# LayerNorm of a convolution module in one sweep per half, weight splits issued at other places, the last convolution behind the first products of the next matrix

## The chip, the cores and the metric

The kernel runs on one core of one Trainium2 chip. The metric is the device time of one execution in microseconds. One profiled execution of the kernel before is read here; its times are counted from the first instruction of the span.

## What is computed

A two-layer decoder trunk on 512 tokens of width 1024, all in float32. Layer 0 is a mixer, layer 1 a causal Conformer convolution module; each is followed by a convolutional feed-forward (FFN). The change lies in the convolution module of layer 1:

```python
def conformer_conv(h, pw1_w, pw1_b, dw_w, dw_b, ln_g, ln_b, pw2_w, pw2_b):
    a, g = jnp.split(h @ pw1_w + pw1_b, 2, axis=-1)
    y = a * jax.nn.sigmoid(g)
    y = causal_depthwise_conv(y, dw_w, dw_b)            # 31 taps
    y = jax.nn.silu(layer_norm(y, ln_g) + ln_b)         # over the 1024 features
    return y @ pw2_w + pw2_b
# then: x = x + gate * y, a modulated RMSNorm, and the FFN of layer 1
```

## The kernel before

**Layout.** Activations stand feature-major: eight blocks k = 0..7 of 128 features by 512 tokens. The tokens are two halves h = 0, 1 of 256. The LayerNorm works on transposed tiles, `zt[h][i]`: half h, pair i of the feature blocks 2i and 2i+1, as 2 groups (a) of 128 tokens by 256 features.

**Matrix products.** Every float32 product is made of three passes of a rounded high part and a rest (`mm3`, lines 190 to 192). Activations are split into `hi` and `lo` (ACT copies, DVE subtracts). Weights come 1024 rows by 256 columns at a time, in a fixed order of the stream: the eight of pw1, the four of pw2 (called W0 to W3 here), then the FFN's. `pull_raw` loads one as two halves of 512 KB into nine `raw` buffers over SP's queue; `pull_split` (lines 257 and 259) splits one into `whi`/`wlo` (four buffers each, two to a weight) or, with an argument, into `shi`/`slo` in general slots. `next_w(ahead=n)` hands out the next weight and first splits n more.

**The convolution.** `glu_out(k, ...)` forms the gated block `yd` (ACT sigmoid, DVE line 1230) and copies it shifted into `y8` by 16 small DMAs, eight on SP's queue and eight on POOL's (line 1239). `conv_pe(k, h)` does the 31 taps as 64 small matmuls (line 1259) and ends with a DVE add that evacuates the PSUM tile (line 1262). `stat(k)` transposes on TensorE (1269), ACT copies into `zt` (1271), and DVE makes `bn_stats` (1276). The last two blocks, `LAST = (6, 7)`, go by halves of the tokens (lines 1306 to 1329).

**LayerNorm and pw2** (lines 1377 to 1397). `ln_stats(h)` is a chain of small DVE steps that ends with mean and 1/sqrt of the variance. `ln_pair(h, i)` normalises pair i (two DVE operations, line 1356), transposes it back on TensorE (line 1360, tile `zb`), and makes silu (ACT, 1364), `hi` (ACT, 1367) and `lo` (DVE, 1368) for blocks 2i and 2i+1. `pw2_first(h, k)` is block k's share of the products with W0 and W1: 12 matmuls of 256 columns into four PSUM tiles. The loop over n does pair n, and then the products of pair n-1. After it `proj_out` uses W2 and W3, adds the residual, and goes on to the FFN.

**Order.** TensorE's instructions run in the order in which the program writes them, throughout. DVE and ACT keep the written order inside the block of lines 1377 to 1397; outside it a scheduler of the compiler places their instructions, and it also puts instructions written behind the block between those of the block. SP's loads are placed by the scheduler too. Each engine's queue is served in order.

Of the kernel before, what the change touches and what calls it, by code (L numbers as in the profile page):

```python
# [13 lines left out]
ALU = mybir.AluOpType  # L14
# [3 lines left out]
P = 128  # L18
D = 1024
KT = 8  # L20
# [15 lines left out]
CD = (3, 3, 3, 3, 3, 3)  # L36
# [20 lines left out]
def body(ctx, tc, x, c, positions, ada_w, ada_b, norm_mix_g, norm_ffn_g, ab_w_in, a_vnorm_g,  # L57
# [4 lines left out]
    V, A, PE = nc.vector, nc.scalar, nc.tensor  # L62
# [162 lines left out]
    raws, parts = [], []  # L225
# [38 lines left out]
    def pull_split(ks_slots=0):  # L264
        for _ in split_steps(ks_slots):
            pass

    taken = [0]
# [29 lines left out]
    def later(n, f):  # L298
        cnt[0] += 1
        due.append((now[0] + n, cnt[0], f))  # L300
# [661 lines left out]
    def drain(*its):  # L962
        for it in its:
            for _ in it:
                pass
# [253 lines left out]
    z0 = {}  # L1219
# [32 lines left out]
    def conv_pe(k, h=None):  # L1252
        n, i = (256, 0) if h is None else (128, 128 * h)
        cps = psum([P, 2, n], "cv")
        for q in range(4):
            o = 4 * q if not h else 0
            for s in range(8):
                g = 32 * (s % 4)
                PE.matmul(cps[g:g + 32, s // 4, o:], wds[k][q][:, 32 * s:32 * s + 32],  # L1259
                          y8[k][s // 2][:, s % 2, i + o - 4 * q:i + n - 4 * q],  # L1260
                          start=(q == 0 and s < 4), stop=(q == 3 and s > 3), tile_position=(0, g))
        V.tensor_tensor(z0[k][:, :, i:i + n], cps, cdb[:, 2 * k:2 * k + 2, None].to_broadcast([P, 2, n]), op=ALU.add)

    def stat(k, hs=(0, 1)):

# [11 lines left out]

    def conf_post(k, pg, pa):
        glu_out(k, pg, pa)
        later(CD[k], lambda: conv_pe(k))  # L1280
        later(CD[k] + SD[k], lambda: stat(k))

    for j in range(3):
# [21 lines left out]
    wg, wa = next_w(), next_w(ahead=0)  # L1305
    for h in range(2):
        pgs = []
        for i, k in enumerate(LAST):
            ps = psum([P, 256])
            gemm_fm(wg, nrm1.h, i, ps, h=None, acts_h=h)  # L1310
            pgs.append(ps)
            if h == 1 and i == 1:
                conv_pe(LAST[0], 0)
            tick()
        for i, k in enumerate(LAST):
            ps = psum([P, 256])
            if h == 1 and i == 1:
                gemm_fm(wa, nrm1.h, i, ps, last=False, h=None, ks=range(5), acts_h=h)
                stat(LAST[0], (0,))
                stat(LAST[1], (0,))  # L1320
                gemm_fm(wa, nrm1.h, i, ps, first=False, h=None, ks=range(5, 8), acts_h=h)
            else:
                gemm_fm(wa, nrm1.h, i, ps, h=None, acts_h=h)
            glu_out(k, pgs[i], ps, h)
            if h == 1 and i == 0:
                conv_pe(LAST[1], 0)
            tick()
    while due:
        tick()
    while len(raws) < taken[0] + 2:  # L1330
        pull_raw()
    while len(parts) < taken[0] + 1:
        pull_split()
    pull_split(KT)

    sact = [(slot(F32R, name="hi"), slot(F32R, name="lo")) for _ in range(KT)]

# [10 lines left out]
        yield from rsqrt_steps(r, ve, 2)  # L1348
        res += [mv3[:, :, 0], r]

    def ln_pair(h, i, mr):

        mean, r = mr
        for a in range(2):
            t = zt[h][i][:, a].rearrange("p k f -> p (k f)")
            V.tensor_scalar(t, t, mean[:, a:a + 1], r[:, a:a + 1], op0=ALU.subtract, op1=ALU.mult)
        ps = psum([P, 2, 2, P], "zb")
        for e in range(2):
            for a in range(2):
                PE.transpose(ps[:, e, a, :], zt[h][i][:, a, e, :], ident)  # L1360
        for e in range(2):
            k = 2 * i + e
            z = slot(shape=[P, 256], name="z")
            A.activation(z.rearrange("p (n a) -> p n a", a=2), ps[:, e].rearrange("p a n -> p n a"), AF.Silu,
                         scale=colt["lng"][:, k:k + 1], bias=colt["lnb"][:, k:k + 1])
            hi, lo = (hsl(t, h) for t in sact[k])
            A.activation(hi, z, AF.Copy)
            V.tensor_tensor(lo, z, hi.bitcast(F32), op=ALU.subtract)
# [4 lines left out]
    def pw2_first(h, k):  # L1373
        for q in range(4):
            gemm_fm(w2[q // 2], sact, q % 2, pss[q], k == 0, k == KT - 1, h=h, ks=[k])

    with tc.manual_schedule(engines={E.DVE, E.Activation}):
        mr = [[], []]
        drain(ln_stats(0, mr[0]))
        A.activation(small(KT, "junk"), zt[0][0][:, 0, 0, :KT], AF.Silu)  # L1380
        conv_pe(LAST[0], 1)
        for n in range(9):
            h, i = divmod(n, 4)
            if n == 4:
                pw2_first(0, 6)
            if n < 8:
                ln_pair(h, i, mr[h])
            for k in ((2 * n - 2) % 8, (2 * n - 1) % 8) if n else ():
                if (n, k) != (4, 6):
                    pw2_first((n - 1) // 4, k)  # L1390
            if n == 1:
                conv_pe(LAST[1], 1)
            elif n == 2:
                for k in LAST:
                    stat(k, (1,))
            elif n == 3:
                drain(ln_stats(1, mr[1]))
    nrm2 = Norm(1, 3, 4, "nfg")
    pss = proj_out(sact, 1, nrm2, list(range(KT)), pss)
    conv_ffn(1, nrm2, None, pss)  # L1400
# [37 lines left out]
```

## Time and profile before

| | us |
|---|---|
| median of 3 runs (1185.06 to 1185.18) | 1185.12 |
| the profiled execution, whole | 1184.57 |
| its span, first to last instruction | 1182.9 |
| TensorE (PE) busy | 1145.6 (97%) |
| weight loads (PEld) busy | 974.4 (82%) |
| VectorE (DVE) busy | 756.4 (64%) |
| ScalarE (ACT) busy | 461.1 (39%) |
| GpSimd (POOL) busy | 42.4 (4%) |

The page also has the span in 40 equal slices of 29.6 us, with busy tenths of each engine and the clock granted to TensorE. A timeline row has the start, the time from the first start to the last end of a group of like instructions, the engine, the line, the operation with its output and inputs, the count, and in brackets the idle time before it with what ended it.

### The profile page before, as it was taken

The page shows a single profiled execution, that of the slowest core. Times are in us where ns is not written, and L with a number is a line of the kernel's source. Part 1 is how long each engine was busy: PE and PEld are TensorE (multiplying, and loading weights), DVE is VectorE, ACT ScalarE, POOL GpSimd, SP SyncE. Part 2 cuts the span into 40 slices and gives each one's busy share as a digit, 9 for nine tenths or more (in the row PEclk, how much of TensorE's full clock was granted, in tenths as well). Part 3 has the DMA queues.
Part 4 walks back from the last instruction along what each step waited for, and adds up shares of the span by engine and source line. Part 5 has one row for each costly group of instructions (what it writes and reads, how often), then busy time and mean ns, then how long its engine had stood idle before and what let it go on. Part 6 is the DMA issues. An engine that isn't in the chain of part 4 may idle for free.

```text
span 1182.9 us, 17714 instructions
## 1 busy us (share of the span) xinstructions
PE 1145.6 (97%) x6970; PEld 974.4 (82%) x6970; DVE 756.4 (64%) x1370; ACT 461.1 (39%) x714; POOL 42.4 (4%) x90
## 2 busy tenths in 40 slices
PE   5999999999999899999999999699999999999998
PEld 3899787898888788888899779589888888888888
DVE  5898999679788767865447443567765655562221
ACT  3253863355444333422225222453544433341221
POOL 0000000000000000000001324100000000000000
PEclk8999999999999999999999999899999999999999
DMA  9863337615665655576422744321333233223301
GB/s 295 280 194 125 101 120 259 198 55 161 193 190 177 179 177 181 168 231 216 148 91 64 203 132 116 95 65 43 107 107 98 86 101 107 80 80 98 98 18 37
DMA packets 138058, 161.95 MB, mean 137 GB/s; under 512 B 12511, under 2 KB 125175, under 8 KB 137975
## 3 DMA queue, kind: packets, MB, share of 16 engines
q1 hardware_dynamic: 135415, 156.62, 42.8%
q0 software_dynamic: 2560, 4.20, 1.7%
q8 instruction: 55, 0.90, 0.3%
q14 instruction: 28, 0.23, 0.1%
HBM read 150.30 MB, written 2.10 MB: 129 GB/s over the span
## 4 chain that ended last, share of the span: by engine, by line
PE 90%; DVE 6%; ACT 2%; DMA 1%; issue 1%; SPq 0%; DVEq 0%; ACTq 0%
PE ps L190 24%; PE ps L191 24%; PE ps L192 24%; PE ps L986 6%; PE cv L1259 2%; PE gi L190 1%; PE gi L192 1%; PE gi L191 1%; PE g L192 1%; PE g L190 1%; PE g L191 1%; PE y L785 1%; PE zb L1360 1%; PE pT L771 1%; ACT p L753 1%
## 5 line engine op out<-in xcount | busy, mean ns | idle before, releaser
L259 DVE TENSOR_TENSOR wlo<-raw,whi 128x1024 fp32r<-128x1024 f32 (+1 forms) x174 | 207.9, 1198 | 202.2 <-ACT whi L257 199.1
L190 PE MATMUL ps<-hhi,whi 128*128 128x512 f32 (+1 forms) x800 | 307.4, 384 | 0.0
L192 PE MATMUL ps<-hhi,wlo 128*128 128x512 f32 (+1 forms) x800 | 305.3, 382 | 0.0
L191 PE MATMUL ps<-hlo,whi 128*128 128x512 f32 (+1 forms) x800 | 305.2, 381 | 0.0
L257 ACT ACTIVATE whi<-raw 128x1024 fp32r<-128x1024 f32 (+1 forms) x174 | 179.7, 1039 | 319.3 <-PE ps L191 307.2
L190 PE MATMUL ps<-hi,whi 128*128 128x512 f32 (+1 forms) x600 | 207.6, 346 | 0.0
L192 PE MATMUL ps<-hi,wlo 128*128 128x512 f32 (+1 forms) x600 | 204.8, 341 | 0.0
L191 PE MATMUL ps<-lo,whi 128*128 128x512 f32 (+1 forms) x600 | 204.8, 341 | 0.0
L190 PEld LDWEIGHTS ps<-hhi,whi 128*128 128x128 f32 x800 | 150.8, 189 | 32.7 <-issue 3.2
L192 PEld LDWEIGHTS ps<-hhi,wlo 128*128 128x128 f32 x800 | 150.7, 188 | 28.9
L191 PEld LDWEIGHTS ps<-hlo,whi 128*128 128x128 f32 x800 | 150.9, 189 | 28.4
L190 PEld LDWEIGHTS ps<-hi,whi 128*128 128x128 f32 x600 | 113.9, 190 | 14.3 <-issue 1.2
L192 PEld LDWEIGHTS ps<-hi,wlo 128*128 128x128 f32 x600 | 113.9, 190 | 12.9
L191 PEld LDWEIGHTS ps<-lo,whi 128*128 128x128 f32 x600 | 114.0, 190 | 12.5
L1083 DVE SCALAR_TENSOR_TENSOR acc<-ps,cols,acc 128x511 f32<-128x511 f32 x88 | 65.3, 746 | 49.3 <-ACT acc L1081 49.3
L1081 ACT ACTIVATE acc<-ps,cols,cols 128x512 f32<-128x512 f32 x88 | 67.1, 770 | 71.8 <-PE ps L192 63.0
L641 DVE SCALAR_TENSOR_TENSOR aacc<-raw,cact,aacc 128x1024 f32<-128x1024 f32 x70 | 89.6, 1280 | 0.7
L1084 DVE SCALAR_TENSOR_TENSOR acc<-ps,cols,acc 128x510 f32<-128x510 f32 x88 | 65.5, 748 | 2.5
L1239 POOL DMA_DIRECT2D y<-yd x80 | 40.5, 539 | 450.4 <-issue 391.4
L1100 ACT ACTIVATE acc<-acc 128x512 f32<-128x512 f32 x44 | 27.6, 630 | 64.7 <-DVE acc L1084 64.6
L190 PE MATMUL gi<-whi,hhi 128*128 128x256 f32 x160 | 45.9, 287 | 0.0
L191 PE MATMUL gi<-wlo,hhi 128*128 128x256 f32 x160 | 45.3, 283 | 0.0
(241 smaller groups left out, 1368.3 us busy)
## 6 DMA issues: line engine op xcount, KB each, us to landing
raw<-in_ffn_up_w_dram SPq DMA_DIRECT2D x88, 512.0 KB, 3.8
raw<-in_ada_w_dram SPq DMA_DIRECT2D x80, 512.0 KB, 4.6
raw<-in_ffn_down_w_dram SPq DMA_DIRECT2D x40, 512.0 KB, 3.5
raw<-in_conv_pw_w_dram SPq DMA_DIRECT2D x24, 512.0 KB, 3.5
adaw<-in_ada_w_dram SPq DMA_DIRECT2D x32, 256.0 KB, 6.0
raw<-in_ab_w_in_dram SPq DMA_DIRECT2D x14, 512.0 KB, 6.8
raw<-in_ab_w_out_dram SPq DMA_DIRECT2D x8, 512.0 KB
raw<-in_ab_w_in_dram SPq DMA_DIRECT2D x12, 256.0 KB, 6.3
```

Source lines behind the costliest of these rows:

```text
L190: PE.matmul(ps, l[0], r[0], start=start, stop=False)
L191: PE.matmul(ps, l[0], r[1], start=False, stop=False)
L192: PE.matmul(ps, l[1], r[0], start=False, stop=stop)
L257: A.activation(hi[:, :n, :], part, AF.Copy)
L259: V.tensor_tensor(lo[:, :n, :], part, hi.bitcast(F32)[:, :n, :], op=ALU.subtract)
L641: V.scalar_tensor_tensor(acc, raw, cact[:, k:k + 1], acc, op0=ALU.mult, op1=ALU.add)
L986: PE.matmul(hsl(pss[q], h), ws[q // 2][k][u][:, q % 2 * P:(q % 2 + 1) * P], r, start=(k == 0 and r is hi and u == 0), stop=(k == KT - 1 an ...
L1081: A.activation(acc, ps, AF.Identity, bias=colt["fdb"][:, 44 * l + m:44 * l + m + 1], scale=fdw(l, 2, m))
L1083: V.scalar_tensor_tensor(acc[:, 1:], ps[:, :S - 1], fdw(l, 1, m), acc[:, 1:], op0=ALU.mult, op1=ALU.add)
L1084: V.scalar_tensor_tensor(acc[:, 2:], ps[:, :S - 2], fdw(l, 0, m), acc[:, 2:], op0=ALU.mult, op1=ALU.add)
L1100: A.activation(acc, acc, AF.Silu)
L1239: queue.dma_start(y8[k][s // 2][64 * a:64 * a + 64, s % 2, o:o + n // 2], bass.AP(tensor=src.tensor, offset=src.offset + 1 + o, ap=[src.ap ...
```

## The change

The convolution's closing add becomes a step of its own (`conv_pe` returns it). The split of W0 into slots is issued ahead of the second half of the last two pw1 blocks, that of W1 into `whi`/`wlo` inside it, and that of W2 inside the hand-ordered block, in the second half of the LayerNorm. `ln_pair` is cut into `ln_norm(h)` (all four pairs of a half), `ln_back(h, i)` (transposes) and `ln_silu(h, i, ps)`. The loop is replaced by an order written out: the convolution of block 6 stands first on TensorE with its add behind the norms, that of block 7 behind the products of blocks 0 and 1.

```diff
-        V.tensor_tensor(z0[k][:, :, i:i + n], cps, ...)
+        return lambda: V.tensor_tensor(z0[k][:, :, i:i + n], cps, ...)
...
     for h in range(2):
         pgs = []
+        if h == 1:
+            while len(raws) < taken[0] + 2:
+                pull_raw()
+            pull_split(KT)
...
             if h == 1 and i == 1:
-                conv_pe(LAST[0], 0)
+                conv_pe(LAST[0], 0)()
+                pull_split()
...
-    while len(raws) < taken[0] + 2:
+    while len(raws) < taken[0] + 3:
         pull_raw()
-    while len(parts) < taken[0] + 1:
-        pull_split()
-    pull_split(KT)
...
         mr = [[], []]
+        add = conv_pe(LAST[0], 1)
         drain(ln_stats(0, mr[0]))
         A.activation(small(KT, "junk"), zt[0][0][:, 0, 0, :KT], AF.Silu)
-        conv_pe(LAST[0], 1)
-        for n in range(9):
...
+        ln_norm(0)
+        add()
+        b = [ln_back(0, 0), ln_back(0, 1)]
+        ln_silu(*b[0])
+        ln_silu(*b[1])
+        pw2_first(0, 0)
+        pw2_first(0, 1)
+        b = [ln_back(0, 2)]
+        add = conv_pe(LAST[1], 1)
+        add()
+        ln_silu(*b[0])
+        pw2_first(0, 2)
+        for k in LAST:
+            stat(k, (1,))
+        b = [ln_back(0, 3)]
+        it = ln_stats(1, mr[1])
+        next(it)
+        ln_silu(*b[0])
+        for k in (3, 4, 5):
+            pw2_first(0, k)
+        drain(it)
+        ln_norm(1)
+        pw2_first(0, 6)
+        b = [ln_back(1, 0)]
+        pw2_first(0, 7)
+        for i in range(4):
+            ln_silu(*b[i])
+            if i < 3:
+                b.append(ln_back(1, i + 1))
+            if i == 1:
+                pull_split()
+            for k in (2 * i, 2 * i + 1):
+                pw2_first(1, k)
```

## Rows read from the trace of the kernel before

**Rows 1.** The page: the span, and TensorE's granted clock in 40 slices, in tenths.

```profile
span 1182.9 us, 17714 instructions
...
PEclk8999999999999999999999999899999999999999
```

**Rows 2.** Stretches: length, busy us (count) by engine, granted clock, DMA share, GB/s.

```profile
743.34:746.86 3.52, 0.01 (x1) 0.03 (x1) 3.35 (x13) 0.00 (x0) 1.56 (x4) 1.00 0.58 138
746.86:753.70 6.84, 3.96 (x17) 3.39 (x18) 2.10 (x6) 3.44 (x8) 0.00 (x0) 0.51 0.75 240
753.70:788.03 34.33, 28.92 (x277) 26.91 (x276) 15.01 (x45) 13.73 (x29) 0.00 (x0) 1.00 0.06 16
788.03:840.00 51.97, 51.69 (x368) 48.63 (x367) 40.12 (x92) 24.57 (x42) 0.00 (x0) 1.00 0.27 82
```

**Rows 3.** Waits of PE from 735 to 790: total us, times, longest.

```profile
PE zb L1360 <- DVE zt L1356: 11.8, 6, 3.5
```

**Rows 4.** Timeline of PE, 738.6 to 788.6.

```profile
740.92 2.42 PE L1259 MATMUL cv<-y,w8d 128*32 128x128 f32 x56 [0.29 <-DMA y<-yd]
...
746.86 1.13 PE L1360 MATMUL zb<-ident,zt 128*128 128x128 f32 x4 [3.52 <-DVE zt L1356]
...
764.37 0.78 PE L1360 MATMUL zb<-ident,zt 128*128 128x128 f32 x4 [1.72 <-DVE zt L1356]
...
774.34 0.78 PE L1360 MATMUL zb<-ident,zt 128*128 128x128 f32 x4 [1.46 <-DVE zt L1356]
...
778.00 0.78 PE L1360 MATMUL zb<-ident,zt 128*128 128x128 f32 x4
...
781.67 0.78 PE L1360 MATMUL zb<-ident,zt 128*128 128x128 f32 x4
...
788.03 0.40 PE L190 MATMUL ps<-hi,whi 128*128 128x512 f32 x1
```

**Rows 5.** Timeline of DVE, 739 to 747: the first half's statistics.

```profile
739.24 0.75 DVE L1276 BATCH_NORM_STATS2 lnst<-zt 128x6 f32<-128x256 f32 x2
739.90 0.66 DVE L1230 SCALAR_TENSOR_TENSOR yd<-ps,cols,sg 128x256 f32<-128x256 f32 x1
740.39 0.69 DVE L259 TENSOR_TENSOR slo<-raw,shi 128x512 fp32r<-128x512 f32 x1
740.99 0.26 DVE L1342 BATCH_NORM_AGGREGATE lnmv<-lnst 128x2 f32<-128x24 f32 x1
...
743.22 1.23 DVE L259 TENSOR_TENSOR wlo<-raw,whi 128x1024 fp32r<-128x1024 f32 x1
...
746.31 0.73 DVE L1356 TENSOR_SCALAR zt<-zt,lnmv,lnr 128x256 f32<-128x256 f32 x2
```

**Rows 6.** Timeline of DVE, 767 to 773: the second half's statistics.

```profile
767.48 0.38 DVE L1342 BATCH_NORM_AGGREGATE lnmv<-lnst 128x2 f32<-128x24 f32 x2
...
770.12 0.73 DVE L1356 TENSOR_SCALAR zt<-zt,lnmv,lnr 128x256 f32<-128x256 f32 x2
772.54 0.43 DVE L1368 TENSOR_TENSOR lo<-z,hi 128x256 fp32r<-128x256 f32 x1 [1.69 <-ACT hi L1367]
```

**Rows 7.** Timeline of ACT, 771 to 776: two pairs.

```profile
771.49 0.56 ACT L1364 ACTIVATE z<-zb,cols 128x256 f32<-128x256 f32 x1 [4.39 <-PE zb L1360]
...
772.99 0.42 ACT L1367 ACTIVATE hi<-z 128x256 fp32r<-128x256 f32 x1
```

**Rows 8.** SP's queue, and the landing of line 1239's DMAs.

```profile
740.81 6.02 SPq L1239 DMA_DIRECT2D y<-yd  x8
746.93 54.69 SPq L238 DMA_DIRECT2D raw<-in_ffn_up_w_dram  x9
...
DMA to landing us min/median/max: 1.9/3.2/4.9
```

**Rows 9.** Timeline of DVE, 723 to 730.

```profile
723.64 1.28 DVE L1246 TENSOR_TENSOR w8d<-e,w 128x512 f32<-128x512 f32 x2
728.34 1.22 DVE L259 TENSOR_TENSOR wlo<-raw,whi 128x1024 fp32r<-128x1024 f32 x1 [3.43 <-ACT whi L257]
```

More of the change, by code (lines that the diff above doesn't have):

```diff
@@ L1261, in conv_pe @@
                           start=(q == 0 and s < 4), stop=(q == 3 and s > 3), tile_position=(0, g))
-        V.tensor_tensor(z0[k][:, :, i:i + n], cps, cdb[:, 2 * k:2 * k + 2, None].to_broadcast([P, 2, n]), op=ALU.add)
+        return lambda: V.tensor_tensor(z0[k][:, :, i:i + n], cps,
+                                       cdb[:, 2 * k:2 * k + 2, None].to_broadcast([P, 2, n]), op=ALU.add)
     def stat(k, hs=(0, 1)):
@@ L1279, in conf_post @@
         glu_out(k, pg, pa)
-        later(CD[k], lambda: conv_pe(k))
+        later(CD[k], lambda: conv_pe(k)())
         later(CD[k] + SD[k], lambda: stat(k))
@@ L1325, in body @@
             if h == 1 and i == 0:
-                conv_pe(LAST[1], 0)
+                conv_pe(LAST[1], 0)()
             tick()
@@ L1349, in ln_stats, with ln_norm, ln_back @@
         res += [mv3[:, :, 0], r]
[L1351 to L1356, printed above, removed]
+    def ln_norm(h):
+        mean, r = mr[h]
+        for i in range(4):
+            for a in range(2):
+                t = zt[h][i][:, a].rearrange("p k f -> p (k f)")
+                V.tensor_scalar(t, t, mean[:, a:a + 1], r[:, a:a + 1], op0=ALU.subtract, op1=ALU.mult)
+    def ln_back(h, i):
         ps = psum([P, 2, 2, P], "zb")
@@ L1360, in ln_pair, with ln_silu @@
                 PE.transpose(ps[:, e, a, :], zt[h][i][:, a, e, :], ident)
+        return h, i, ps
+    def ln_silu(h, i, ps):
         for e in range(2):
@@ L1378, in body @@
         mr = [[], []]
+        add = conv_pe(LAST[0], 1)
         drain(ln_stats(0, mr[0]))
         A.activation(small(KT, "junk"), zt[0][0][:, 0, 0, :KT], AF.Silu)
-        conv_pe(LAST[0], 1)
-        for n in range(9):
[L1383 to L1397, printed above, removed]
+        ln_norm(0)
[23 more added lines that the diff above has]
+        pw2_first(0, 7)
+        for i in range(4):
+            ln_silu(*b[i])
[5 more added lines that the diff above has]
+                pw2_first(1, k)
     nrm2 = Norm(1, 3, 4, "nfg")
```

## The prediction

> **What bounds the kernel now.** The page comes first: the span is 1182.9 us, and TensorE's granted clock stands at 9 tenths in every slice but the first and the 26th, which read 8 [rows 1]. So TensorE runs nearly without a break, and one place other than the start is weak: slice 26 of 29.6 us each covers about 739 to 769 us, the LayerNorm between pw1 and pw2. The stretches show its size [rows 2]: from 753.70 to 788.03 PE is busy 28.92 of 34.33 us, from 746.86 to 753.70 it is busy 3.96 of 6.84 at a granted clock of 0.51, from 743.34 to 746.86 it does nothing; in the 52 us that follow it is busy 51.69 of 51.97. The change can gain only what is lost in that stretch. The table of waits names the loss in one row: PE stood before the back transposes (`zb`) for 11.8 us in six waits, each ended by a norm on DVE [rows 3]. The timeline of PE shows them one by one, the longest 3.52 us ahead of the first pair [rows 4].
>
> Two causes lie behind the six. The first wait is the statistics of half 0. There DVE takes 5.32 us from the first bn_aggr (740.99) to the first norm (746.31) [rows 5]; in half 1 the same chain takes 2.64 us (767.48 to 770.12) [rows 6]. The difference of 2.68 us is weight splits between its steps: three `slo`, and the `wlo` at 743.22, with the evacuation of the convolution. One more `slo` of 0.60 us stands ahead of the bn_aggr (740.39 to 740.99). The other waits come from the loop: pair n+1 is normed only when DVE has served pair n's `lo`, which waits for ACT. From the first transpose (770.68, which is 0.56 after the norm's start) to the first `lo` (772.54) go 1.86 us [rows 6], and PE has only the products of one pair to put there.
>
> **The change part by part.** *Splits.* The steps of ACT and DVE stay the same in number (four small and two large for W0 and W1, two large for W2). W0's four `slo` of about 0.69 us, 2.8 in all, go ahead of the second half; there DVE stands idle for 3.43 us before the `wlo` at 728.34 [rows 9], and the slots, unlike `whi` and `wlo`, hold no weight that is still in use, so I cost them at nothing. If that cover failed they would push the gate `yd` by up to 2.8 us. W1 takes the place in time that W0's `whi`/`wlo` has now, from 727 us. W2's two `wlo` go into half 1, where DVE has room (15.01 busy of 34.33 us [rows 2]). Their loads change too: W2's two raw buffers come free at about 768; today the second is free at 743.22 + 1.23 = 744.5 [rows 5]. So SP's loads of the FFN weights behind them start later; see the third rival.
>
> *The first wait.* Without splits in the chain the first norm comes 3.3 us earlier (2.68 + 0.60), at 743.0, or at 742.4 if bn_stats too moves up by the 0.6 us for which a `wlo` held it. The transposes can follow 0.56 us later, at 743.0 to 743.6. TensorE then still has the convolution of block 6, whose 56 recorded last matmuls end at 740.92 + 2.42 = 743.34 and which was paced by DMAs [rows 4]; these copies are not moved. So the first transposes start at about 743.5, and the 3.52 us shrink to 0.2.
>
> *All four pairs at once.* Eight norms take 4 x 0.73 = 2.9 us [rows 6] in place of 0.73 before the first transposes. It costs nothing for the first pair, whose transposes wait for its own two norms, but the first `lo` is queued behind them: by ACT it would be due at 743.5 + 1.86 = 745.4; DVE is through with the norms at about 745.6 and with the add of the convolution (0.4) at 746.0, so `lo` ends at 746.4 and PE starts the products at about 746.5. PE has two groups of transposes to fill 743.5 to about 745.0. A gap of 1.1 to 1.9 us is left; I take 1.4.
>
> *After that.* PE has products in hand for each later wait. ACT needs 1.92 us a pair (771.49 to the end of `hi` at 773.41 [rows 7]) and PE 3.66 (774.34 to 778.00, the same to 781.67, where its rows show no wait [rows 4]), so ACT keeps ahead. Two places are near. The convolution of block 7 now stands behind two blocks of products and one group of transposes, 746.5 + 2.9 + 0.8 = 750.2. Its copies leave SP from 740.8 at the latest over 6.02 us; the last of eight is issued at 746.1 and lands 1.9 to 4.9 us later, 3.2 in the median [rows 8]: 748.0 to 751.0, most likely 749.3. Wait 0 to 0.8, taken as 0. The add for it on DVE has two `lo` of pair 2 and bn_stats queued behind it; who wants them is PE after one more block. The norm of half 1: the statistics' transposes end near 754, ACT copies (0.7) and serves pair 3 (1.92) to 756.7, its last `lo` ends at 757.2, 2.64 us of chain and 0.56 to the transposes make 760.4; PE has block 2, the statistics' transposes, pair 3's and blocks 3 to 6 until about 760.6. Wait 0 to 0.6, taken as 0.
>
> *PSUM.* Four tiles for the sums, two for the statistics' transposes, one for the convolution and one for a pair make the eight that the program has; the trace of before shows no wait for a tile. One of a pair is free when ACT has read it, within the 1.92 us above, so I take 0, and 0.5 as the upper bound.
>
> *The clock.* Before, the clock fell to half (1.2 of 2.4 GHz) after PE had stood still for 3.52 us, and stayed there for 6.84 us [rows 2]; the later gaps of up to 1.72 us left it at full speed [rows 4, 2]. A gap of 1.4 us is inside the latter. What half speed cost: at most half of PE's busy 3.96 us, 1.98; at least the two groups of transposes at 1.13 in place of 0.78 [rows 4], 0.7. Products lie in it as well, and they are dense, so I take 1.6, nearer the upper end.
>
> **The sum.** Waits: 11.8 before, 0.2 + 1.4 = 1.6 after, a gain of 10.2 to 10.3; with the clock's 1.6 it is 11.9 us. The profiled execution, 1184.57, would become 1172.7; the median of the runs lies 0.55 above the profiled one, so the forecast is 1173.2 us. Behind the block nothing is late: PE was already full there [rows 2], and W3's second half waits for the end of the products as it did. With both ends of each term (gap 1.1 to 1.9, clock 0.7 to 1.98, the near waits 0 to 1.9) the gain is 8.6 to 12.6, that is 1172.5 to 1176.5, and some tenths lower where two groups of transposes in a row cost less than 0.8 each.
>
> **The rivals.** *The clock falls all the same.* PE is thinly used from 739 to 741 us and has two short bursts and a gap until 746.5; if that counts as rest, the dense products after it run at half speed for as long as before, 6.84 us [rows 2], and lose half of that, 3.4 us, where I counted none: 1176.6. For it speaks that the fall before came in this very place; against it, that 3.52 us of standstill preceded it and that gaps of 1.46 and 1.72 us did nothing [rows 4]. The Trainium skill, "TensorE: Matmul & The Clock Gate", section "A second HAM failure mode: psum-queue depth-cycling", says that PE which idles shortly and often between groups of matmuls swings between the two clock levels. By that rule this rival would be the case; the trace here does not bear it out for half 1, where such gaps stood at 1.00. Chance 0.14.
>
> *The splits stay in the chain.* The scheduler places what stands outside the block, and today it puts W2's split, written behind the block, into the chain. If it did so with another split, the 3.3 us come back, PE stands still as now and the clock falls: 11.9 - 3.3 - 1.6 = 7.0 us gain, 1178.2. Against it: W2's split is now bound to its place, W3's has to wait for W1's buffers, and W0's has its own idle stretch. Chance 0.06.
>
> *Slower: the FFN's weights come late.* Place: SP's queue, served in order. The loads behind W2's buffers start about 25 us later, and nine loads share the 54.69 us from 746.93 [rows 8]. If they are needed as soon as they land, PE waits up to 25 us at the first FFN products, and the kernel takes 1185.1 - 11.9 + 25 = 1198 us; it is slower once that wait exceeds 14 us (11.9 and the 2.4 that a measurement can tell). Against it: four halves, two whole weights, are in before W2's by the buffers of W0 and W1, which now come free earlier; PE had no wait in the 52 us behind the block, and the DMA engines stood at a share of 0.27 there [rows 2], so there is room to catch up. Chance 0.03.
>
> **How the numbers follow.** The forecast has 0.70, the fallen clock 0.14, splits in the chain 0.06, late weights 0.03; 0.07 are left for an order of the scheduler that gives back some of the gain behind the block, half of it within 0.2% (2.4 us, about what a measurement of this kernel can tell from no change). The range takes the forecast's bounds, with 1.3 us below them for the cheaper transposes, and the clock rival: 1171.2 to 1177.0; the splits' rival, the late weights and the rest are left out. Faster by over 0.2%: 0.70 + 0.14 + 0.06 + 0.03 = 0.93; within 0.2%: 0.04; slower: 0.03.
>
> **What would show it.** In the profile after: no L259 between bn_aggr and the first norm on DVE, and the first norm before 743.5; eight norms in a row of some 2.9 us; the row "PE zb <- DVE zt" at under 1 us; one gap of 1 to 2 us ahead of the first pw2 product, ended by a `lo`; the granted clock at 1.00 from 740 to 780; the first 512-column product behind the block at about 776. The forecast would be wrong if the convolution of block 7 waited for its copies by more than a microsecond, if the clock fell, or if the first 512-column product came at 776 and the end did not move with it: then the gain was given back in the FFN.

## The result and the profile after

The changed kernel takes 1172.3 us in the median (1171.4 to 1173.4) where the kernel before took 1185.15: a ratio of 0.9887, with a 95% interval of 0.987 to 0.9904. It is faster by 1.1%, and the whole interval lies below 1. The forecast was 1173.2 us. The profiled execution took 1171.4 us, 13.17 less than that of before.

The page of the changed kernel; the first and the 26th slice, which stood at 8 [rows 1], are at 9:

```profile
span 1169.7 us, 17707 instructions
...
PEclk9999999999999999999999999999999999999999
```

Its stretches, with the columns of [rows 2] (length, busy us and count of PE, PEld, DVE, ACT and POOL, granted clock, DMA share, GB/s), the last two now parted at the new end of the block:

```profile
743.34:746.86 3.52, 2.78 (x53) 2.15 (x45) 2.63 (x8) 1.57 (x4) 2.16 (x4) 1.00 0.76 214
746.86:753.70 6.84, 6.84 (x105) 6.47 (x106) 2.37 (x6) 3.87 (x9) 0.00 (x0) 1.00 0.11 20
753.70:774.86 21.16, 21.16 (x182) 21.16 (x179) 14.03 (x39) 12.70 (x26) 0.00 (x0) 1.00 0.24 76
774.86:828.00 53.14, 52.86 (x373) 49.61 (x372) 41.47 (x93) 25.18 (x42) 0.00 (x0) 1.00 0.26 80
```

PE is busy throughout from 746.86 to the end of the block at 774.86, and the clock is at its upper level. All the waits of PE between 735 and 790 us (total, times, longest) are now these:

```profile
PE cv L1259 <- DMA y<-yd: 1.7, 3, 1.2
PE ps L190 <- ACT hi L1378: 0.7, 1, 0.7
```

The row of 11.8 us [rows 3] is gone. In its place stand 0.7 us ahead of the first product, where 1.4 were forecast, and 1.7 us ahead of the convolution of block 6 (0.5 before), which were not. PE's timeline of the changed kernel shows both (in brackets the idle time and what ended it):

```profile
740.51 0.82 PE L1259 MATMUL cv<-y,w8d 128*32 128x128 f32 x4 [1.18 <-DMA y<-yd]
...
742.44 2.16 PE L1259 MATMUL cv<-y,w8d 128*32 128x128 f32 x56 [0.41 <-DMA y<-yd]
...
744.53 1.09 PE L1367 MATMUL zb<-ident,zt 128*128 128x128 f32 x8
...
746.29 0.39 PE L190 MATMUL ps<-hi,shi 128*128 128x256 f32 x1 [0.67 <-ACT hi L1378]
...
750.12 1.96 PE L1259 MATMUL cv<-y,w8d 128*32 128x128 f32 x64
...
774.86 0.40 PE L190 MATMUL ps<-hi,whi 128*128 128x512 f32 x1
```

On DVE no split (L259) stands any more between the first bn_aggr and the norms, and eight norms follow each other:

```profile
739.45 0.24 DVE L1345 BATCH_NORM_AGGREGATE lnmv<-lnst 128x2 f32<-128x24 f32 x1
...
742.54 2.67 DVE L1360 TENSOR_SCALAR zt<-zt,lnmv,lnr 128x256 f32<-128x256 f32 x8
745.13 0.42 DVE L1262 TENSOR_TENSOR z<-cv,cdb 128x256 f32<-128x256 f32 x1
746.27 0.42 DVE L1379 TENSOR_TENSOR lo<-z,hi 128x256 fp32r<-128x256 f32 x1 [0.72 <-ACT hi L1378]
```

Behind the block the two profiles are alike: from the first 512-column product behind the block to the end of the span it is 394.87 us before (1182.9 - 788.03) and 394.84 after (1169.7 - 774.86). The whole gain lies in the block, and nothing of it is given back.

For the experiments the block is cut in two on PE: from the start of the convolution of block 7's first half (733.58 before, 733.96 after), which stands ahead of everything that changed on PE, to the first pw2 product; and from there to the first 512-column product. Before it is 18.08 + 36.37 = 54.45 us, after 12.33 + 28.57 = 40.90. So 5.75 us were gained ahead of the products and 7.80 within them; 0.38 of the 13.55 are lost because the block begins that much later.

### The profile page after: what moved, and what is told of

It reads as the page before. It is cut to its first block, busy times and chain, and to the rows that moved or that the text cites. A ratio compares the mean times of both kernels' runs of the same rounds, so it can differ in the third digit from the quotient of the medians.

```text
span 1169.7 us, 17707 instructions
## 1 busy us (share of the span) xinstructions
PE 1142.1 (98%) x6970; PEld 973.3 (83%) x6970; DVE 756.4 (65%) x1370; ACT 460.6 (39%) x714; POOL 42.9 (4%) x90
## 4 chain that ended last, share of the span: by engine, by line
PE 90%; DVE 4%; DMA 3%; ACT 2%; issue 1%; SPq 1%; DVEq 0%; ACTq 0%
PE ps L190 24%; PE ps L191 24%; PE ps L192 24%; PE ps L986 6%; PE cv L1259 2%; DMA adaw<-in_ada_w_dram 1%; PE gi L190 1%; PE gi L191 1%; PE gi L192 1%; PE y L785 1%; PE g L190 1%; PE g L192 1%; PE g L191 1%; PE pT L771 1%; ACT p L753 1%
## 5 line engine op out<-in xcount | busy, mean ns | idle before, releaser
L259 DVE TENSOR_TENSOR wlo<-raw,whi 128x1024 fp32r<-128x1024 f32 (+1 forms) x174 | 207.7, 1198 | 201.0 <-ACT whi L257 196.9
L191 PEld LDWEIGHTS ps<-lo,whi 128*128 128x128 f32 x600 | 113.7, 190 | 12.5
```

Source lines behind the costliest of these rows:

```text
L191: PE.matmul(ps, l[0], r[1], start=False, stop=False)
L259: V.tensor_tensor(lo[:, :n, :], part, hi.bitcast(F32)[:, :n, :], op=ALU.subtract)
```

## The experiments

All of them at a glance. The two lengths are from one profiled execution each, the time is a median, the ratio is to the kernel before on the same chip.

| kernel | to the first product | from there to the end | sum | us | ratio, 95% interval |
|---|---|---|---|---|---|
| before | 18.08 | 36.37 | 54.45 | 1185.15 | |
| changed | 12.33 | 28.57 | 40.90 | 1172.3 | 0.9887 [0.987, 0.9904] |
| e1 splits back | 15.31 | 30.26 | 45.57 | 1175.29 | 0.9925 [0.9904, 0.9946] |
| e2 splits only | 16.25 | 41.62 | 57.87 | 1188.34 | 1.0024 [1.0012, 1.0036] |
| e3 norm by pair | 12.80 | 35.39 | 48.19 | 1179.44 | 0.9955 [0.9937, 0.9972] |
| e4 filler | 17.73 | 37.50 | 55.23 | 1185.07 | 0.9998 [0.9988, 1.0007] |
| e5 addition first | 15.83 | 30.20 | 46.03 | 1174.28 | 0.9903 [0.9888, 0.9918] |
| e6 W2 loose | 14.63 | 28.59 | 43.22 | 1172.5 | 0.9887 [0.9873, 0.9902] |
| e7 splits only, W2 last | 19.20 | 37.30 | 56.50 | 1186.08 | 1.0003 [0.9993, 1.0012] |
| e8 convolution 7 early | 17.52 | 26.16 | 43.68 | 1173.53 | 0.9896 [0.988, 0.9913] |
| e9 loads behind copies | 11.02 | 29.06 | 40.08 | 1170.45 | 0.9877 [0.9862, 0.9891] |
| e10 copies 10 and 6 | 11.15 | 28.93 | 40.08 | 1170.07 | 0.9867 [0.9851, 0.9884] |
| e11 copies and order | 11.08 | 28.89 | 39.97 | 1170.79 | 0.988 [0.9865, 0.9895] |
| e12 changed, again | 15.09 | 28.58 | 43.67 | 1172.99 | 0.9899 [0.9883, 0.9916] |

**The parts undone one by one.** e1 is the changed kernel with the splits of the kernel before.

```diff
-        if h == 1:
-            while len(raws) < taken[0] + 2:
-                pull_raw()
-            pull_split(KT)
...
-                pull_split()
...
-    while len(raws) < taken[0] + 3:
+    while len(raws) < taken[0] + 2:
         pull_raw()
+    while len(parts) < taken[0] + 1:
+        pull_split()
+    pull_split(KT)
...
-            if i == 1:
-                pull_split()
```

> The changed kernel with the splits of W0, W1 and W2 issued where they were before; the new order of norms, transposes and products stays. Theory (the splits lengthen the chain of half 0 and the clock follows the standstill): the first norm comes 3.3 us later than the 742.54 of the changed kernel, at about 745.8, the first transposes at 746.4 in place of 744.53, so 1.9 us are lost; PE stands still for about 3 us before them, the clock falls to half for some 6.8 us and up to 3.4 us more are lost: 1174.2 us if the clock holds, 1177.6 if it falls. Rival (the convolution of block 6 paces the start anyway, so where the splits lie does not matter): 1172.3 us, the clock at 1.00.

It took 1175.29 us, 3.0 more, between the two values of the theory (1174.2 and 1177.6). On its DVE the splits are back in the chain, and the norms begin at 745.53 instead of 742.54:

```profile
740.42 0.25 DVE L1343 BATCH_NORM_AGGREGATE lnmv<-lnst 128x2 f32<-128x24 f32 x1
740.59 0.63 DVE L259 TENSOR_TENSOR slo<-raw,shi 128x512 fp32r<-128x512 f32 x1
...
742.65 1.22 DVE L259 TENSOR_TENSOR wlo<-raw,whi 128x1024 fp32r<-128x1024 f32 x1
...
745.53 2.67 DVE L1358 TENSOR_SCALAR zt<-zt,lnmv,lnr 128x256 f32<-128x256 f32 x8
```

PE stands for 2.92 us, and the clock falls: its first eight transposes read

```profile
746.08 1.99 PE L1365 MATMUL zb<-ident,zt 128*128 128x128 f32 x8 [2.92 <-DVE zt L1358]
```

where the changed kernel's take 1.09. Half of these 0.9 us disappears in a shorter wait for `hi` (0.25 instead of 0.67): from the first transposes to the first product it is 2.24 us here and 1.76 there. With the 1.69 us more from the first product to the end, the fallen clock costs 0.5 + 1.7 = 2.2 us here. So the 3.0 us are not the price of the longer chain alone.

e2 does the opposite: the kernel before with the splits moved and nothing else.

```diff
+        if h == 1:
+            while len(raws) < taken[0] + 2:
+                pull_raw()
+            pull_split(KT)
...
+                pull_split()
...
-    while len(raws) < taken[0] + 2:
+    while len(raws) < taken[0] + 3:
         pull_raw()
-    while len(parts) < taken[0] + 1:
-        pull_split()
-    pull_split(KT)
...
+            elif n == 6:
+                pull_split()
```

> The kernel before with the splits moved as in the change and nothing else (that of W2 in the loop at pair 2 of half 1). Theory: DVE's chain of half 0 is short, but the evacuating add of block 6's convolution still stands before the first norm on DVE and waits for the convolution (end at 743.3 to 744.5), so the first transposes come at about 744.3 to 745.5 in place of 746.86; the clock holds, which gives 1.6 us; the waits of the later pairs stay: a gain of 3 to 4 us, 1181 to 1182. Rival (the splits carry most of the change's gain): below 1177. Rival (they carry nothing): 1185.

It took 1188.34 us: not 3 to 4 us faster but 2.8 slower than before (1185.52 on the same chip). Two reasons are on its DVE. The chain ends early, but ahead of the norm stands the addition, which waits for the convolution; and W2's split stands ahead of the last pair's norm:

```profile
743.65 0.42 DVE L1262 TENSOR_TENSOR z<-cv,cdb 128x256 f32<-128x256 f32 x1 [2.59 <-PE cv L1259]
743.99 0.73 DVE L1358 TENSOR_SCALAR zt<-zt,lnmv,lnr 128x256 f32<-128x256 f32 x2
...
779.66 2.36 DVE L259 TENSOR_TENSOR wlo<-raw,whi 128x1024 fp32r<-128x1024 f32 x2 [0.52 <-ACT whi L257]
781.94 0.73 DVE L1358 TENSOR_SCALAR zt<-zt,lnmv,lnr 128x256 f32<-128x256 f32 x2
```

e3 keeps the changed kernel's splits and order, but each pair is normalised only just ahead of its transposes (those of half 0's first two pairs together).

```diff
-    def ln_norm(h):
+    def ln_norm(h, pairs=range(4)):
...
-        ln_norm(0)
+        ln_norm(0, (0, 1))
...
+        ln_norm(0, (2,))
...
+        ln_norm(0, (3,))
...
-        ln_norm(1)
+        ln_norm(1, (0,))
...
+                ln_norm(1, (i + 1,))
```

> The changed kernel with each pair's two norms right before its transposes on DVE (the first two pairs of half 0 together) in place of all four pairs at once. Theory (what the sweep buys is that no norm queues behind the lo of another pair): norms wait again behind lo and bn_stats, PE waits before the transposes of pair 3 of half 0 (about 2 us) and of pair 1 of half 1 (about 1.5 us), with some tenths at three others: about 4.4 us lost, 1176.7. Rival (transposes issued one pair ahead on PE are enough, the sweep itself is worth nothing): 1172.3 to 1173.

It took 1179.44 us, 7.1 more than the changed kernel; 4.4 were expected. Nearly all of it lies behind the first product (35.39 against 28.57 us). The row of waits is back with 3.2 us only (two waits, 1.72 and 1.45), so the rest is elsewhere: in the distance from pair to pair, which is 3.7 us in half 1 as it was before, and in a fall of the clock behind the wait of 1.72 us (0.84 from 753 to 760 us, 0.94 from 760 to 770; microsecond by microsecond it is one fall, at 0.50 from 758 to 761). From the transposes behind this wait to those of half 1's first pair it takes 7.88 us (757.27 to 765.15) where the changed kernel takes 6.18 (753.98 to 760.16): 1.7 us for the fall. PE's timeline of e3:

```profile
768.63 0.78 PE L1367 MATMUL zb<-ident,zt 128*128 128x128 f32 x4 [1.45 <-DVE zt L1360]
...
772.30 0.78 PE L1367 MATMUL zb<-ident,zt 128*128 128x128 f32 x4
...
776.00 0.78 PE L1367 MATMUL zb<-ident,zt 128*128 128x128 f32 x4
```

**The clock by itself.** e4 is the kernel before with 24 transposes, which nothing reads, between the convolution of block 6 and the first back transposes.

```diff
         conv_pe(LAST[0], 1)
+        dm = psum([P, 4, P], "dm")
+        for j in range(24):
+            PE.transpose(dm[:, j % 4, :], ident, ident)
```

> The kernel before with 24 transposes of the identity, which nobody reads, issued on PE between the convolution of block 6 and the first back transposes, where PE stands still for 3.52 us; about 3 us of work. Theory (the half clock is the standstill's doing and costs 1.6 us): the clock stays at 1.00 and the kernel takes 1183.5 us. Rival (the fall of the clock costs nothing, because DVE and ACT set the pace there anyway): 1185.1 us with the clock at 1.00. Third: the clock falls all the same, 1185.1 us.

It took 1185.07 us, the same as before (the interval takes in 1). The filler did its work on PE and the wait behind it fell from 3.52 us to 1.23; but in the next one, 2.88 us ahead of pair 1, the clock went down (0.97 from 749 to 750 us, 0.50 from 750). PE's timeline of e4 has this first group of transposes:

```profile
747.64 0.78 PE L1360 MATMUL zb<-ident,zt 128*128 128x128 f32 x4 [1.23 <-DVE zt L1356]
```

and these are its stretches behind it, in the columns of [rows 2]:

```profile
747.00:753.00 6.00, 2.48 (x12) 2.11 (x13) 2.31 (x7) 2.38 (x5) 0.00 (x0) 0.75 0.78 237
753.00:760.00 7.00, 6.16 (x86) 5.75 (x84) 1.63 (x5) 1.32 (x4) 0.00 (x0) 0.73 0.12 36
```

So this run doesn't isolate the price of the clock; it shows that the fall doesn't hang on the one wait in front, which the sum had tied it to. A second fall, at 0.50 from 767 to 770 us, followed the wait of 1.72 us ahead of pair 3.

**The order on DVE and PE.** e5 moves one step of the changed kernel: the addition stands ahead of the norms.

```diff
-        ln_norm(0)
         add()
+        ln_norm(0)
```

> The changed kernel with one step moved on DVE: the addition that empties the convolution of block 6 (L1262) stands ahead of the eight norms of half 0 instead of behind them. Theory (the place of this addition is part of the gain): it waits for the convolution, which ended at about 744.5 us in the changed kernel, so the norms run from 745.0 to 747.7, the first transposes begin at 745.6 (744.53 with the norms first) and the first lo is through at 748.1 (746.3). The products begin 1.5 to 1.9 us later: 1174.0 us if the clock holds at 1.00, about 1176 if it falls. Rival (only the splits and the norms of four pairs matter): 1172.3 us.

1174.28 us: 2.0 more than the changed kernel, inside what the theory gave, but with intervals that overlap; against e12, the changed kernel run again, it is 1.3. Its four executions (1173.66 to 1175.41) lie above seven of the eight that the changed kernel has in the two runs. The chain is through at 741.30, and then DVE waits 4.51 us for the convolution, while all four pairs are queued behind the addition:

```profile
741.14 0.16 DVE L157 SCALAR_TENSOR_TENSOR lnr<-rw,rn 128x2 f32<-128x2 f32 x1
745.82 0.42 DVE L1262 TENSOR_TENSOR z<-cv,cdb 128x256 f32<-128x256 f32 x1 [4.51 <-PE cv L1259]
746.16 2.67 DVE L1360 TENSOR_SCALAR zt<-zt,lnmv,lnr 128x256 f32<-128x256 f32 x8
```

e6 gives up the bound place of W2's split in the changed kernel.

```diff
-            if i == 1:
-                pull_split()
```

> The changed kernel without its bound place for the split of W2; it is left to the last product that needs it, and the two large wlo go where the scheduler finds room, one ahead of bn_stats and one behind bn_aggr of half 0. Theory (a split in the chain of statistics costs its own time): two times 1.23 us on DVE put the norms of half 0 from 742.5 to about 745.0 us and the first product from 746.3 to about 748.3: 1174.3 us if the clock holds, 1176 to 1177 if it falls. Rival (the place of W2's split doesn't matter, or its earlier loads give it back): 1172.3 us.

1172.5 us: the same, as the rival had it. The two `wlo` did go into the chain (one ahead of bn_stats, one behind bn_aggr), and the norms began at 742.77. But PE could not have used them sooner:

```profile
739.98 1.53 PE L1259 MATMUL cv<-y,w8d 128*32 128x128 f32 x8 [2.21 <-DMA y<-yd]
741.85 3.50 PE L1259 MATMUL cv<-y,w8d 128*32 128x128 f32 x56 [0.33 <-DMA y<-yd]
745.28 1.09 PE L1367 MATMUL zb<-ident,zt 128*128 128x128 f32 x8
```

The convolution of block 6 ends at about 745.3, and the norms of the first pair were there at 743.5 (742.77 and the 0.73 of two norms [rows 6]). The statistics have slack now; the convolution has none. Whether W2's place matters where the copies come sooner, as in e9, was not run.

e7 is e2 with W2's split behind the last pair's `lo`.

```diff
-            elif n == 6:
+            elif n == 7:
                 pull_split()
```

> The kernel before with the splits moved as in the run with the moved splits alone (1188.3 us), but W2's split stands behind the last pair's lo, where in that run it stood ahead of the last pair's norm. Theory (that run was slower than before since W2's two wlo, 2.36 us, and the steps of ACT behind them held up the last pair, and PE's halt there let the clock fall): 2.4 to 3.5 us less for the wait and up to 1.5 for the clock, 1183 to 1186, I say 1184.5 us; the first 512-column product at about 787. Rival (it was slow by falls of the clock between the pairs, which this leaves alone): 1188 us.

1186.08 us, between the two expectations: the place of W2's split was worth 2.3 us of e2's excess. What is left is no gain at all over the kernel before. The row of waits stands at 8.0 us in five waits, and a second row shows what else was lost:

```profile
PE zb L1362 <- DVE zt L1358: 8.0, 5, 2.9
PE cv L1259 <- DMA y<-yd: 3.3, 2, 3.0
```

The convolution of block 6 waited 3.3 us for its copies here and 1.6 in e2, 0.5 in the kernel before. So e2 and e7 show what the moved splits bring together with later copies; what they would bring with the copies in time was not run.

e8 puts the convolution of block 7 ahead of the first products.

```diff
+        add = conv_pe(LAST[1], 1)
         pw2_first(0, 0)
         pw2_first(0, 1)
...
-        add = conv_pe(LAST[1], 1)
         add()
```

> The changed kernel with one step moved on PE: the convolution of block 7 stands ahead of the products of blocks 0 and 1 instead of behind them and the transposes of pair 2. Theory (its copies are late and the products hide that): SP issues the last copy at about 748.0 us and it lands 1.9 to 3.2 us later, so PE waits for y<-yd until 750 to 751 and the first product begins at 750.5 instead of 746.3; the 2 us of the convolution itself are spent within that wait and save as much behind it. Net 2.3 to 3 us with the clock at 1.00: 1175 us; with the clock fallen in the wait 1177 to 1178. Rival (the copies come in time, the place is free): 1172.3 us.

1173.53 us: 1.2 more than the changed kernel, half of what the theory gave, with intervals that overlap. The copies were nearly in time: PE waited 0.24 and 0.27 us for them.

```profile
748.35 2.53 PE L1259 MATMUL cv<-y,w8d 128*32 128x128 f32 x56 [0.27 <-DMA y<-yd]
750.81 0.38 PE L190 MATMUL ps<-hi,shi 128*128 128x256 f32 x1
```

The first product comes later, but 26.16 us end the block where 28.57 did: the convolution is only paid at another place. Against e12, whose convolution of block 6 waited for its copies in the same way, the block has the same length (43.68 and 43.67 us). So no gain of this order is shown.

**The copies.** In e5, e6 and e8 the convolution of block 6 waited 2.0 to 2.2 us for its copies in one piece, and ran for the greater part at half clock behind. In the changed kernel three weight loads stand ahead of these copies in SP's queue, one more than before (with the splits put back, in e1, there are two), since W0's buffers come free earlier. Its SP queue:

```profile
731.68 1.63 SPq L238 DMA_DIRECT2D raw<-in_ffn_up_w_dram  x3
734.86 6.07 SPq L1239 DMA_DIRECT2D y<-yd  x8
```

e9 puts three of the four loads around these copies behind the last one; one load stays ahead.

```diff
+    copied = newest(mybir.EngineType.SP)
     while len(raws) < taken[0] + 3:
         pull_raw()
...
+    with after(copied):
+        while len(raws) < taken[0] + 4:
+            pull_raw()
     nrm2 = Norm(1, 3, 4, "nfg")
```

> The changed kernel with four FFN weight loads of SP's queue moved: two raw that stood ahead of the copies of block 6 and one between those of block 6 and 7 now follow the last copy. Theory (in the changed kernel the first gate of the block is no longer the statistics but the convolution of block 6, held up by its copies, and the loads ahead of them hold up the copies): SP needs 5.1 to 5.6 us for the eight copies, as it does with two loads ahead, in place of 6.1 to 7.7 with three; the convolution ends at about 743.4 instead of 744.5, PE waits less than 1 us for y<-yd, the clock stays at 1.00 from 737 to 747, the first product begins about 0.7 us earlier: 1171.3 us against 1172.3. Rival 1 (the time of the copies has nothing to do with the loads): 1172.3 us, with waits for y<-yd of 1.7 us and more. Rival 2 (the FFN's weights, now loaded later, are late): slower than 1173.

e12 is the changed kernel again, on the same chip.

> The changed kernel unaltered, beside the three others on the same chip: 1172.3 us. Theory (its spread comes from the wait for the copies ahead of the convolution of block 6 and a fall of the clock behind it): where the profile shows one wait for y<-yd of 2 us or more, the clock is below 1.00 between 737 and 747 us and the execution takes 1172.5 to 1173.5; where the waits are split up, as in the profile shown, it is 1.00 and 1171.4. Rival (the spread lies elsewhere): the stretch from 737 to 747 looks the same in a slower execution.

e9 took 1170.45 us, e12 1172.99. PE's timeline of e9 at this convolution:

```profile
740.78 0.63 PE L1259 MATMUL cv<-y,w8d 128*32 128x128 f32 x8
741.66 3.05 PE L1259 MATMUL cv<-y,w8d 128*32 128x128 f32 x56 [0.25 <-DMA y<-yd]
744.65 1.39 PE L1368 MATMUL zb<-ident,zt 128*128 128x128 f32 x8
```

and that of e12:

```profile
743.47 1.51 PE L1259 MATMUL cv<-y,w8d 128*32 128x128 f32 x8 [2.31 <-DMA y<-yd]
745.31 3.88 PE L1259 MATMUL cv<-y,w8d 128*32 128x128 f32 x56 [0.34 <-DMA y<-yd]
```

In e12 one wait of 2.31 us stands ahead of the convolution, and its last 56 matmuls take 3.88 us where the changed kernel's first profile has 2.16 and the clock at 1.00. This profiled execution took 1175.99 us, more than the 1173.5 that the theory allowed and 4.59 more than the first one: 2.77 are in the block (43.67 against 40.90), 1.83 before it, where the block began later. So the theory holds for the block's share, and the spread has a second place outside it: on the pages, the first and the 15th slice of the clock stand at 8 in e12 and at 9 in the changed kernel's first profile. What each of them costs was not measured. In e9 no wait of more than 0.25 us is left ahead of the convolution. SP issued its copies only a little faster (11.57 us for sixteen, 5.8 for eight, against 6.07 and 6.77 for block 6 in the two profiles of the changed kernel; expected 5.1 to 5.6), so the expected way was only partly right: with one load ahead, they land in time.

e10 adds to e9 another share of the copies, e11 adds to e10 another order of the norms.

```diff
-            for a, queue in enumerate((nc.gpsimd, nc.sync)):
+            for a, queue in enumerate((nc.gpsimd, nc.gpsimd if h and s in (3, 7) else nc.sync)):
```

> As the run with the loads behind the copies, and besides two of SP's eight copies of the second half of blocks 6 and 7 go through POOL's queue (10 and 6 instead of 8 and 8; POOL needed 4.03 us for eight, SP 6.07). Theory (the copies set the first gate): POOL is through in about 5.0 us and SP in about 4.2, so the last copy leaves 1 us earlier still and the convolution ends at about 742.5; from there on the eight norms (742.5 to 745.2) and the addition set the first lo at 745.6, so only 0.3 us come of it: 1171.0 us. Rival (the gate is elsewhere): same as the run with the loads alone.

```diff
-        ln_norm(0)
+        ln_norm(0, (0, 1, 2))
         add()
         b = [ln_back(0, 0), ln_back(0, 1)]
         ln_silu(*b[0])
+        ln_norm(0, (3,))
```

> As the run with 10 and 6 copies, and besides the norms of pair 3 of half 0 stand behind the first two lo on DVE instead of ahead of the addition. Theory (with the copies early, DVE's eight norms gate the first lo): the addition ends at 744.9 and the first lo at 745.3 instead of 746.0, the products begin 0.5 us earlier: 1170.5 us. Rival (ACT's silu and hi, 1 us behind the transposes, gate it anyway): 1171.0 us.

1170.07 and 1170.79 us; the lengths to the first product are 11.02, 11.15 and 11.08 us, so neither edit moved it: the rivals were right. In e11 PE waits 0.5 us for `hi` ahead of the first product, that is for ACT behind the transposes.

The three kernels with the loads behind the copies can be taken together: their twelve executions have a median of 1170.45 us (1168.06 to 1172.23) against 1172.99 (1170.93 to 1175.99) for e12's four on the same chip. That is about 2.5 us, and the best version found here, though the interval of each single one overlaps that of the changed kernel.

## Why the prediction was right, point by point

**The sum.** The forecast took 11.9 us off the profiled execution; 13.17 came off. The block's end was put at about 776 and came at 774.86: 0.2 us of the difference lie ahead of the first product (746.5 forecast, 746.29 measured), the rest behind it. In the rows, the waits fell from 12.3 us (11.8 for the norms, 0.5 for the copies) to 2.4 (0.7 and 1.7): 9.9 where the forecast had 10.2. The clock's 1.6 and 0.7 of the pairs, both below, make 12.2 of the block's 13.55; the other 1.3 lie in shorter distances, such as the 0.53 us from a group of transposes to its first product before (774.34 to 774.87), 0.35 after (762.04 to 762.39). (With its own terms the range of the gain comes to 8.5 to 12.5, a tenth below the 8.6 to 12.6 of the forecast.) That the total came so near is in part luck: the copies came out 1.2 us worse, the gap ahead of the products 0.7 better and the pairs 0.7 better than the sum had them, and the first profile is one in which the clock did not fall.

**The splits.** The chain is as foreseen: the first norm at 742.54 (742.4 to 743.0 forecast), and e1 puts the price of the old place at 3.0 us with the fallen clock in it, where the rival of the splits had 3.3 + 1.6 = 4.9. But the step gave the 3.3 us to the splits alone. In e2 and e7 they brought nothing by themselves: in the old order the addition ahead of the norm waits for the convolution, and the convolution for copies that the moved splits had made later. How much of it is the addition's and how much the copies' is not parted there; with the norms in one sweep the addition's place is 1.3 to 2.0 us (e5). And W2's part is nothing (e6), as long as the copies come that late. The rival that a split would stay in the chain did not come. W0's `slo` went to 729.87 to 733.5, not into the idle 724 to 727.5 that I had named; `yd` followed them at 734.14 and had waited for PE last, so no harm came of it.

**The convolution of block 6.** Here a step was wrong: "these copies are not moved" was true of their code and not of their queue. With one more load ahead, they left SP at 734.86 and the convolution ended at about 744.5, not 743.34. The step that looked at the queues looked only at the loads behind W2's buffers. It cost 1.0 us of the first transposes, hidden in part, by luck, since the gap that I had put behind them shrank with it (1.4 forecast, 0.67 measured). By e9 against the changed kernel this is worth about 2 us, though their intervals overlap; the three kernels with moved loads together give 2.5 against e12.

**All four pairs at once.** The sweep cost nothing ahead of the products in the first profile: the gap was ended by ACT's `hi`, not by a `lo` held up behind the norms as forecast, since the transposes came 1.0 us later and DVE was through with norms and addition at 745.55, 0.72 us before `hi` let it go on. Where the copies come in time the forecast's order shows: in e9 PE waits 0.5 us for `hi` and then 0.6 for `lo`. That the sweep pays is shown by e3, 7.1 us.

**The pairs.** This is the term of the sum that was too small. I read PE as full where the old half 1 went from pair to pair in 3.66 us without a wait in the rows [rows 4]. In the changed kernel the same work takes 3.31. The old distance was the circle of one pair through DVE, PE and ACT: norms at 773.78, transposes at 774.34, `lo` until 777.5, the next norms at 777.45. PE's own rows hide the difference, because matmuls overlap (the products of the pairs are 0.28 us long and start 0.12 us apart): busy PE and PEld (second and third column) over two pairs read so before

```profile
774.34:781.67 7.33, 7.28 (x57) 6.69 (x57) 3.00 (x9) 4.53 (x9) 0.00 (x0) 1.00 0.01 3
```

and so after

```profile
762.04:768.66 6.62, 6.62 (x58) 6.62 (x57) 4.54 (x8) 6.09 (x12) 0.00 (x0) 1.00 0.10 26
```

PE was busy for 7.28 of 7.33 us and still had 0.7 to give (7.33 against 6.62); the weight loads, 6.69, show nearly all of it. The Trainium skill says as much ("Trainium Kernel Development and Optimization", section "Performance Expectations"): the busy time of matmuls is a poor measure of how near a kernel is to its bound, since they are pipelined, and the busy share of the weight loads is one of two good ones. The trace agrees: 6.69 of 7.33 before, 6.62 of 6.62 after. Two such steps are 0.7 of the 1 us that came behind the first product beyond the forecast, and e3, where the 3.7 us return, is slower by more than its listed waits in part for the same reason.

**The clock.** It stayed at 1.00 from 740 to 780 us, as forecast. The term of 1.6 us can be read from the kernel before itself. PE's timeline there has the same work, one group of transposes and the products of two blocks, once behind the fall and once at full clock:

```profile
750.87 1.14 PE L1360 MATMUL zb<-ident,zt 128*128 128x128 f32 x4 [2.88 <-DVE zt L1356]
...
755.65 1.95 PE L1259 MATMUL cv<-y,w8d 128*32 128x128 f32 x64
758.56 0.78 PE L1360 MATMUL zb<-ident,zt 128*128 128x128 f32 x4 [0.96 <-DVE zt L1356]
...
762.05 0.60 PE L1269 MATMUL zT<-ident,z 128*128 128x128 f32 x4
```

That is 4.78 us against 3.49. With the 0.35 us of the first pair's transposes (1.13 against 0.78 [rows 4]) the fall cost 1.6 us. In e1 it cost 2.2; e4 could not isolate it.

The rival, a fall all the same, did not come in the profiled execution, but it is real: it came in e5, e6, e8 and e12, one step earlier than I had placed it, in the wait for the copies. e12 is the changed kernel itself. Of its eight executions in the two runs, the five with a mean granted clock of 0.996 took 1170.93 to 1172.63 us and the three with 0.990 to 0.993 took 1173.4 to 1175.99; the profile first shown is one of the five. Nor was the premise safe that a gap of 1.72 us does nothing: it came from one profile. The same wait of 1.72 us, ahead of pair 3 of half 0, was followed by a fall in all four other kernels that have it (0.83, 0.85 and 0.85 from 760 to 770 us in e2, e4 and e7, 0.84 from 753 to 760 in e3). That other executions of the kernel before fall there too is likely but not shown.

What the Trainium skill reports of another kernel and stood beside this rival ("TensorE: Matmul & The Clock Gate", section "A second HAM failure mode: psum-queue depth-cycling": PE that idles shortly and often between groups of matmuls swings between the levels) fits the old loop better than I allowed: e2 stood at 0.72, 1.00, 0.83, 1.00 and 0.83 in five stretches from 747 to 790 us. The changed kernel has no such gaps left behind the first product and stays at 1.00 there; e3, which has two of them again, fell.

**The near waits.** None came: the convolution of block 7 began at 750.12 (750.2 forecast) without one, and by e8 its place matters little; half 1's norms began at 758.92 and their transposes had no wait; no wait for a PSUM tile appeared.

**The late FFN weights.** This rival did not come. The loads behind W2's buffers did come later (twelve from 766.83 us), and PE lost nothing: the 394.84 us behind the block are those of before. The room was there, as the DMA share of 0.26 says; e9, which delays three more half-weight loads, is no slower either.

## What to carry to other kernels

Where an engine waits for several things in one place, taking one away moves the wait to the next: look for the second gate (here the addition on DVE, then the copies on SP) before crediting the first, and list what else moves up in a queue when buffers come free earlier. A loop that passes through three engines and has the period of its latency looks like a full PE; compare the weight loads' busy time with the length of the stretch, and break the loop by doing one engine's part for all rounds at once. A trace of one execution shows whether a wait was in one piece or in three, and the next execution may differ: look at a second profile before calling a short wait harmless.

## What the hardware showed that was not expected

A wait in three pieces (1.18, 0.16 and 0.41 us) left the granted clock at 1.00; waits of 1.96 to 3.04 us in one piece at the same place (e5, e6, e7, e8, e12) were each followed by microseconds at 0.50 (from 743 us in e5, 742 in e6 and e8, 744 in e7, 746 in e12). One wait of 1.65 us in e2 left it at 1.00 too, so whether the pieces or the length decide is not told apart. A wait of 1.72 us at one other place went both ways: at full clock before [rows 4], with a fall behind it in e2, e3, e4 and e7. The last 56 matmuls of the same convolution took 2.16 us in one execution of the changed kernel and 3.88 in another; not all of that is the clock, for in e9 they took 3.05 at 1.00.

Eight copies of 32 KB from SP's queue took 6.1 to 7.7 us to issue in the kernels with three weight loads of 512 KB ahead of them, 5.1 to 6.0 with two; with one load they took 5.8, so the count of loads is not the only thing at work. PE's waits for the copies ahead of block 6's convolution sort by that count more clearly: 0.2 to 0.6 us in all with one load ahead or two, 1.6 to 3.3 with three. How the loads delay the landing stays open.
